# A Conformer's norm issued ahead of the attention, probabilities scaled on GpSimd, evictions issued behind the weight splits

## The chip, the cores and the metric

One core of a Trainium2 chip runs one decoder layer for 256 tokens. The metric is the device time of one execution in microseconds, the median of several runs. TensorE does the matmuls; VectorE, ScalarE and GpSimd do the elementwise work; SP issues most of the loads. Each engine works through its instructions in the order in which the kernel issued them, and waits where one needs the result of another engine.

## What is computed

`x` is 256 x 2048. A layer is an RMS norm, one input projection, two parallel branches, an output projection with a residual, then an RMS norm, a gated MLP with a 3-tap convolution, another residual and a final RMS norm.

```python
proj = rms_norm(x, mix_norm_g) @ w_in
q, kv, gate_logits, conv_in = split(proj)            # 1024, 1536, 48, 2048 columns
attn = nsa_attention(q, kv, sigmoid(gate_logits), ...)
a, gate = split(conv_in)                             # the Conformer's branch
u = causal_depthwise_conv(a * sigmoid(gate), conv_w, conv_b)     # 31 taps, 1024 channels
conv = silu(layer_norm(u, conv_ln_g, conv_ln_b))
x = x + concat(attn, conv) @ w_out
x = x + conv_glu_ffn(rms_norm(x, ffn_norm_g))
return rms_norm(x, final_norm_g)
```

The attention has 16 query heads and three branches for each: over compressed keys, over selected blocks (with 256 tokens there are four blocks, and all are selected) and over a window, which covers everything. Each branch is a softmax with a bias by distance, and a gate.

## The kernel before

**Weights.** They come in 186 chunks of up to 128 x 2048 float32 in the order of their use: 0 to 15 the pairs of gate and value columns of the Conformer (gb and ab of j = 0 to 7), 16 to 19 the keys and values to be compressed, 20 to 23 the keys, 24 and 25 values, 26 to 29 values and gates (narrower, 128 x 1216), 30 to 37 the queries, 38 to 53 the output projection, then the MLP. Chunks 0 and 1 come with x transposed in one packed input, `head`, cut by `CUTS` into pieces. For accuracy each product is made of three matmuls, high x high, high x low and low x high: `w_split` copies a chunk to `wh` in a rounded type on ScalarE (L109) and subtracts for `wl` (L114), in two halves each, on VectorE or, for chunks within `POOLED`, on GpSimd. The last half issues the load of the chunk three further on SP's queue. `w_next` is called at the start of a chunk and queues the pieces of the split of the chunk two further on; `w_pump` issues them.

**Hooks.** A chunk has four hooks between its matmuls (L323). A hook issues one piece of a split, one entry of `steps` and of `conf`, the attention's ticks that `TICKS` names, and then `fill` issues taps of the Conformer's convolution while a clock of planned VectorE time is less than a lead ahead of the planned TensorE time. `mm3`, `mm_rows`, `attn_tick`, `step` and the evictions charge these two clocks. The convolution has 8 x 31 pieces (`side`): one of ScalarE (L358) and 30 taps of VectorE (L363) for each j, between SBUF and one of two halves of PSUM banks.

**Evictions.** After a chunk's matmuls the kernel issues what empties its PSUM bank: `glu_gate` and `glu` for the Conformer, the multiplications for `tok` (L424), the split of the keys (L487 to L494), `v_evac` (L502), `q_evac` (L552 to L557).

**The norm of x.** `xr` is x in rows; `x_rstd` sums squares on ScalarE (L251) and VectorE (L252), GpSimd takes the power -0.5 (L256), `x_diag` and `x_spread` bring it to all partitions (`rB`). It stands behind chunk 0 and 1.

**The attention.** 32 units (8 query pairs, 2 heads, 2 branches) go through a pipeline of ticks: scores (TensorE), minimum with bias (VectorE, L632), exponential (ScalarE, L643), reciprocal times gate (VectorE, L651), scaling (ScalarE, L658) at D_S = 3, transpose (TensorE, L664) into bank 6 and its eviction `es` (ScalarE, L669) at D_T = 4, product with the values (TensorE, L677, L678) at D_T + 1. The compressed branch (`cmp_scores`, `cmp_exp`, `cmp_probs`, `cmp_tr`, which makes `pct`) goes through `steps`.

**The Conformer's norm.** `conf_steps` fills `conf`: sums over channels (VectorE, L713), means by a matmul (L717) and a copy (`ck`, ScalarE, L741), subtraction (L744), squares (L748), sums, variance by a matmul (L724), power on GpSimd (L754), diagonals (L730), spread by a matmul (L733), multiplication. The list starts when no taps are left and `cbst["q"]` says that the first two query chunks are out. `conf2` holds swish and split, issued in the output projection.

## Time and profile before

| | |
|---|---|
| device time, median of 3 runs | 1143.84 us (1143.76 to 1145.13) |
| the profiled execution: device time | 1145.46 us |
| the profiled execution: span from first to last instruction | 1143.3 us |
| mean granted TensorE clock | 0.993 of full speed |

The spans of TensorE's instructions are modelled in part: matmuls overlap, so a stretch can be shown as wholly busy. Times in the rows are microseconds, means of one instruction nanoseconds. PE is TensorE, PEld its weight loads, DVE VectorE, ACT ScalarE, POOL GpSimd.

### The profile page before, as it was taken

What the parts mean: (1) busy time and instruction counts of PE and PEld (TensorE: products, weight loads), DVE (VectorE), ACT (ScalarE), POOL (GpSimd) and SP (SyncE); (2) the same over time, 40 slices, a digit from 0 to 9 for tenths busy, and PEclk for the clock granted to TensorE, in tenths of its full rate; (3) what the DMA queues carried; (4) which work ended last, traced back from release to release, by engine and by line L of the source; (5) the groups of instructions that cost most, each with busy time, mean ns of one, the idle gap of its engine ahead of it and who ended that gap; (6) DMA issues with size and microseconds to landing.
All of it is one profiled execution on the core that took longest, in us unless ns stands there. A gap on an engine that the chain in (4) does not pass through costs nothing.

```text
span 1143.3 us, 16193 instructions
## 1 busy us (share of the span) xinstructions
PE 1116.6 (98%) x6482; PEld 977.6 (86%) x6482; DVE 767.7 (67%) x1250; ACT 598.3 (52%) x898; POOL 128.3 (11%) x80
## 2 busy tenths in 40 slices
PE   8999999899899999999999999999999999999997
PEld 8999999888778888888888888888888888888886
DVE  6688659676454667777777777777778755456554
ACT  6544255788864555544555554455555444444443
POOL 1988654000000000000000000000000000000000
PEclk9999999999999999999999999999999999999999
DMA  9585416222265465555555555555555555555541
GB/s 374 193 299 201 165 45 247 93 75 74 74 237 205 148 234 195 197 184 185 186 190 197 197 187 184 185 189 193 197 194 184 184 184 184 187 183 187 186 177 74
DMA packets 32279, 207.44 MB, mean 181 GB/s; under 512 B 3867, under 2 KB 6187, under 8 KB 8012
## 3 DMA queue, kind: packets, MB, share of 16 engines
q1 hardware_dynamic: 28592, 199.64, 48.9%
q10 hardware_dynamic: 3612, 6.76, 1.6%
q8 instruction: 51, 0.84, 0.3%
q14 instruction: 24, 0.20, 0.1%
HBM read 204.27 MB, written 2.12 MB: 181 GB/s over the span
## 4 chain that ended last, share of the span: by engine, by line
PE 87%; ACT 5%; DVE 4%; DMA 2%; issue 1%; POOL 1%; DVEq 0%; POOLq 0%; ACTq 0%
PE bank L957 28%; PE bank L959 14%; PE bank L145 9%; PE bank L144 9%; PE bank L146 9%; PE bank L139 4%; PE bank L137 4%; PE bank L138 4%; DMA xr<-in_x 2%; ACT wh L109 1%; PE bank L437 1%; ACT e L643 1%; DVE wl L114 1%; PE bank L677 1%; ACT e L658 1%
## 5 line engine op out<-in xcount | busy, mean ns | idle before, releaser
L109 ACT ACTIVATE wh<-wraw 128x2048 fp32r<-128x2048 f32 (+2 forms) x239 | 355.9, 1505 | 356.5 <-issue 149.6
L114 DVE TENSOR_TENSOR wl<-wraw,wh 128x2048 fp32r<-128x2048 f32 (+1 forms) x185 | 362.6, 1968 | 189.8 <-ACT wh L109 189.7
L957 PE MATMUL bank<-xt,wh 128*128 128x512 f32 x1408 | 488.6, 394 | 0.0
L959 PE MATMUL bank<-xt,wl 128*128 128x256 f32 x1408 | 390.0, 277 | 0.0
L957 PEld LDWEIGHTS bank<-xt,wh 128*128 128x128 f32 x1408 | 264.0, 188 | 61.1
L959 PEld LDWEIGHTS bank<-xt,wl 128*128 128x128 f32 x1408 | 264.4, 188 | 0.0
L137 PE MATMUL bank<-xt,wh 128*128 128x256 f32 x512 | 147.8, 289 | 1.7 <-ACT wh L238 1.7
L139 PE MATMUL bank<-xt,wl 128*128 128x256 f32 x512 | 146.3, 286 | 1.9 <-POOL wl L114 1.6
L138 PE MATMUL bank<-xt,wh 128*128 128x256 f32 x512 | 146.1, 285 | 0.0
L144 PE MATMUL bank<-wh,gh 128*128 128x512 f32 (+1 forms) x360 | 140.8, 391 | 0.0
L145 PE MATMUL bank<-wl,gh 128*128 128x512 f32 (+1 forms) x360 | 140.8, 391 | 0.0
L146 PE MATMUL bank<-wh,gl 128*128 128x512 f32 (+1 forms) x360 | 140.8, 391 | 0.0
L114 POOL TENSOR_TENSOR wl<-wraw,wh 128x1024 fp32r<-128x1024 f32 (+1 forms) x54 | 120.9, 2277 | 36.0 <-ACT wh L109 35.6
L137 PEld LDWEIGHTS bank<-xt,wh 128*128 128x128 f32 x512 | 99.0, 193 | 3.5 <-ACT wh L238 2.1
L139 PEld LDWEIGHTS bank<-xt,wl 128*128 128x128 f32 x512 | 99.0, 193 | 2.5 <-POOL wl L114 1.8
L138 PEld LDWEIGHTS bank<-xt,wh 128*128 128x128 f32 x512 | 99.0, 193 | 0.6
L173 POOL TENSOR_TENSOR rstd<-ms,half 128x1 f32<-128x1 f32 x4 | 2.2, 548 | 857.3 <-DVE ms L166 857.3
L363 DVE SCALAR_TENSOR_TENSOR bank<-us,cw,bank 128x256 f32<-128x256 f32 x232 | 93.7, 482 | 4.7 <-ACT bank L358 4.3
L920 DVE SCALAR_TENSOR_TENSOR yt<-u,vecs,yt 128x255 f32<-128x255 f32 (+1 forms) x176 | 80.9, 481 | 3.1
L144 PEld LDWEIGHTS bank<-wh,gh 128*128 128x128 f32 x360 | 67.8, 188 | 15.8
L145 PEld LDWEIGHTS bank<-wl,gh 128*128 128x128 f32 x360 | 67.8, 188 | 15.8
L146 PEld LDWEIGHTS bank<-wh,gl 128*128 128x128 f32 x360 | 67.8, 188 | 15.8
(185 smaller groups left out, 1047.4 us busy)
## 6 DMA issues: line engine op xcount, KB each, us to landing
wraw<-in_w_u SPq DMA_DIRECT2D x88, 1024.0 KB, 4.8
wraw<-in_w_d SPq DMA_DIRECT2D x44, 1024.0 KB, 4.8
wraw<-in_w_t SPq DMA_DIRECT2D x30, 1024.0 KB, 5.0
wraw<-in_w_o SPq DMA_DIRECT2D x16, 1024.0 KB, 4.9
wraw<-in_w_vg SPq DMA_DIRECT2D x4, 608.0 KB, 3.5
hb<-in_head SPq DMA_DIRECT2D x2, 1024.0 KB, 9.8
xr<-in_x SPq DMA_DIRECT2D x2, 1024.0 KB, 16.0
wb<-rel_scratch ACTq DMA_DIRECT2D x1, 2048.0 KB, 10.7
```

The source lines that it names most:

```text
L109: nc.scalar.activation(h[:, sl], raw[:, sl], AF.Copy)
L114: (nc.gpsimd if pooled else nc.vector).tensor_sub(l[:, sl], raw[:, sl], h[:, sl].bitcast(F32))
L137: nc.tensor.matmul(ps, wh, xh, start=first, stop=False)
L138: nc.tensor.matmul(ps, wh, xl, start=False, stop=False)
L139: nc.tensor.matmul(ps, wl, xh, start=False, stop=last)
L144: nc.tensor.matmul(ps, xh, wh, start=first, stop=False)
L145: nc.tensor.matmul(ps, xh, wl, start=False, stop=False)
L146: nc.tensor.matmul(ps, xl, wh, start=False, stop=last)
L363: nc.vector.scalar_tensor_tensor(y[:, j] if last else acc[0], us[:, j, k:k + T], cw[:, j, k:k + 1], acc[0], op0=OP.mult, op1=OP.add)
L920: nc.vector.scalar_tensor_tensor(ys[i][:, d:], us_[i][:, :T - d], fcw[:, c, k:k + 1], ys[i][:, d:], op0=OP.mult, op1=OP.add)
L957: nc.tensor.matmul(bk[i], wh[:, k, sl], xt[:, kt].rearrange("p a t -> p (a t)"), start=kt == 0, stop=False)
L959: nc.tensor.matmul(bk[i][:, :T], wl[:, k, sl], xt_h[:, kt], start=False, stop=kt == KD - 1)
```

## The change

`late` holds evictions: they are now issued by the next chunk's `w_next`, behind the split that it queues; for chunks that GpSimd splits, `w_next` issues the whole split at once. `POOLED` moves from 3..29 to 5..31. `head` has six pieces, and the three first chunks are loaded ahead of the rows of x; three small loads move from ScalarE's queue, behind the norm of x, to SP's, behind its rows. The norm of x is issued behind chunk 2. The Conformer's list starts when the taps are out and the last `glu` is issued, with more empty entries; its functions stand earlier in the text, and are otherwise the same. The scaling is on GpSimd, D_T is 5. The queries' split (`q_split`) is issued behind the first tick of the next chunk, and a hook runs ticks before steps. The charges of the clocks are raised. No matmul is added or taken away.

```diff
-POOLED = (3, 30)
-CUTS = ((0, 2), (2, 4), (4, 8), (8, 12), (12, 16))
+POOLED = (5, 32)
+CUTS = ((0, 2), (2, 4), (4, 6), (6, 8), (8, 12), (12, 16))
...
+    late = []
...
         while st["split"] <= min(c + ahead, len(chunks) - 1):
             w_pump()
             w_split(cuts)
-        if cuts == 1:
+        if cuts == 1 or POOLED[0] <= st["split"] - 1 < POOLED[1]:
             w_pump()
+        now = late[:]
+        late.clear()
+        for f in now:
+            f()
         return parts.pop(c)
...
-        clock["pe"] += 0.32
+        clock["pe"] += 0.36
...
-        clock["pe"] += 0.64
+        clock["pe"] += 0.7
...
         def load_small():
-            nc.scalar.dma_start(oh, a["onehot"])
-            nc.scalar.dma_start(rbn[:32], a["rel_slots"])
-            nc.scalar.dma_start(cw, a["conv_vecs"])
+            nc.sync.dma_start(oh, a["onehot"])
+            nc.sync.dma_start(rbn[:32], a["rel_slots"])
+            nc.sync.dma_start(cw, a["conv_vecs"])
...
-        w_dma()
+        for _ in range(3):
+            w_dma()
         xr = [ap.tile([P, D], F32, name=f"xr{t}", tag=tg) for t, tg in enumerate(("y", "us"))]
         for t in range(2):
             nc.sync.dma_start(xr[t], x_rows[:, t])
-        w_dma()
-        w_dma()
+        load_small()
...
+        behind = []
+        cbst = {"q": 0, "done": 0, "glu": False}
...
                 if conf:
-                    clock["dve"] += 0.4
+                    clock["dve"] += 0.9
                     conf.pop(0)()
...
         def hook(i, ticks={}):
-            if i < 2:
-                w_pump(1)
-            step()
             if i in ticks:
                 for _ in range(ticks[i]):
                     attn_tick()
-            if i >= 2:
-                w_pump(1)
+            while behind:
+                behind.pop(0)()
+            w_pump(1)
+            step()
             fill(1.0 if i in ticks else 0.8 if cbst["q"] else 2.0)
-            if not side and cbst["q"] and "b" not in cf:
+            if not side and cbst["glu"] and "b" not in cf:
                 conf_steps()
...
+                first = gb, ab
+                continue
+            tile_chunk(gb)
+            if j == 1:
                 x_rstd()
...
-                load_small()
-                first = gb, ab
-                continue
-            tile_chunk(gb)
-            if j == 1:
-                steps[:0] = [x_diag, lambda: None, x_spread]
                 tile_chunk(ab)
-                glu(0, first[1], glu_gate(first[0]))
-                glu(1, ab, glu_gate(gb))
+                steps[:0] = [x_diag, x_spread, lambda: glu(0, first[1], glu_gate(first[0])),
+                             lambda gb=gb, ab=ab: glu(1, ab, glu_gate(gb))]
             else:
-                sg = glu_gate(gb)
+                sg = []
+                late.append(lambda gb=gb, sg=sg: sg.append(glu_gate(gb)))
                 tile_chunk(ab)
-                glu(j, ab, sg)
+                late.append(lambda j=j, ab=ab, sg=sg: glu(j, ab, sg[0]))
+        late.append(lambda: cbst.update(glu=True))
...
+        def conf_steps():
+            cf["b"] = bank[6][:, 384:]
+            conf.extend((
+                lambda: None, lambda: conf_sum("y", y, 0, P), lambda: conf_sum("y", y, P, T), lambda: None,
+                lambda: None, lambda: conf_mean(0), lambda: conf_mean(1),
+                lambda: (conf_apply(OP.subtract, 0), conf_sq(0)), lambda: conf_apply(OP.subtract, 4),
+                lambda: (conf_sum("s0", cf["s"]), conf_sq(4)), lambda: None, lambda: conf_sum("s1", cf["s"]),
+                lambda: None, lambda: None, conf_var, conf_rstd, lambda: None, lambda: None,
+                lambda: conf_spread(0), lambda: conf_spread(1), lambda: conf_apply(OP.mult, 0),
+                lambda: conf_apply(OP.mult, 4)))
...
-        for n in range(4):
-            tile_chunk(bank[n][:, :T])
+        def k_evac(n):
             br, q = divmod(n, 2)
             k32 = bank[n][:, :T]
             nc.vector.tensor_mul(k32, k32, rB)
...
                 nc.scalar.activation(k_h[h, r, q, br], k32[h], AF.Copy)
                 nc.vector.tensor_sub(k_l[h, r, q, br], k32[h], k_h[h, r, q, br].bitcast(F32))
+            for r in range(2):
+                h, o = slice(64 * r, 64 * r + 64), slice(64 - 64 * r, 128 - 64 * r)
                 nc.scalar.activation(k_h[o, r, q, br], k32[h], AF.Copy)
                 nc.scalar.activation(k_l[o, r, q, br], k_l[h, r, q, br].bitcast(F32), AF.Copy)
+
+        for n in range(4):
+            tile_chunk(bank[n][:, :T])
+            late.append(lambda n=n: k_evac(n))
...
-        for t in range(2):
-            v_evac(t, 0, vb[t][:, :256])
+        late.extend(lambda t=t, src=vb[t][:, :256]: v_evac(t, 0, src) for t in range(2))
...
-                    clock["pe"] += 0.35
+                    clock["pe"] += 0.42
...
+        late.append(vg_evac)
...
+        def q_split(i):
             for r in range(2):
                 h, o = slice(64 * r, 64 * r + 64), slice(64 - 64 * r, 128 - 64 * r)
                 nc.scalar.activation(qs[h, i % 4, r], q32[i][h], AF.Copy)
                 nc.vector.tensor_sub(qs[o, i % 4, r], q32[i][h], qs[h, i % 4, r].bitcast(F32))
+            split_q.add(i)
...
         def st_scale(n):
             i, r, br = units[n]
             e, lsum = US[n]
             for t, (lo, hi, _) in enumerate(HALVES):
-                nc.scalar.activation(e[:, lo:hi], e[:, lo:hi], AF.Copy, scale=lsum[:, br, t:t + 1])
+                nc.gpsimd.tensor_scalar_mul(e[:, lo:hi], e[:, lo:hi], lsum[:, br, t:t + 1])
...
-        D_S, D_T = 3, 4
+        D_S, D_T = 3, 5
...
             clock["pe"] += 1.4
-            clock["dve"] += 0.85
+            clock["dve"] += 1.1
...
+        def q_out(i):
+            q_evac(i, bank[i % 2])
+            behind.append(lambda: q_split(i))
+            if i % 2:
+                cbst["q"] = i // 2 + 1
+                cmp_branch(i // 2)
+
         for i in range(8):
             if i == 2:
                 fill(1e9)
             tile_chunk(bank[i % 2][:, :T], TICKS[min(i, 2)])
-            q_evac(i, bank[i % 2])
-            if i % 2:
-                cbst["q"] = i // 2 + 1
-                cmp_branch(i // 2)
+            late.append(lambda i=i: q_out(i))
```

## Rows read from the trace of the kernel before

**Rows 1.** The page: busy time of the engines over the span, and its group of the first matmul of a gate chunk (busy us, mean ns of one, then idle time before).

```profile
PE 1116.6 (98%) x6482; PEld 977.6 (86%) x6482; DVE 767.7 (67%) x1250; ACT 598.3 (52%) x898; POOL 128.3 (11%) x80
...
L137 PE MATMUL bank<-xt,wh 128*128 128x256 f32 x512 | 147.8, 289 | 1.7 <-ACT wh L238 1.7
```

**Rows 2.** Busy time by stage: the stretch, its length, then busy us and instructions of each engine, TensorE's granted clock, the DMA engines' share and GB/s.

```profile
0.00:30.00 30.00, 25.39 (x172) 24.35 (x173) 17.92 (x41) 20.39 (x38) 5.41 (x12) 0.94 0.88 358
30.00:130.00 100.00, 100.00 (x830) 99.22 (x830) 81.23 (x205) 43.02 (x53) 87.95 (x40) 1.00 0.64 226
142.00:175.00 33.00, 30.70 (x257) 30.18 (x256) 20.35 (x55) 19.08 (x38) 16.52 (x10) 0.95 0.17 58
175.00:199.00 24.00, 24.00 (x186) 24.00 (x186) 23.22 (x49) 12.57 (x24) 10.30 (x9) 1.00 0.71 252
199.00:305.00 106.00, 95.57 (x663) 87.58 (x662) 71.27 (x240) 88.81 (x261) 1.41 (x5) 0.98 0.22 79
```

**Rows 3.** The same view of the three stretches with a granted clock under 1.

```profile
10.00:20.00 10.00, 9.00 (x60) 8.79 (x61) 9.86 (x18) 10.00 (x20) 0.00 (x0) 0.83 1.01 426
160.00:180.00 20.00, 18.00 (x134) 17.80 (x134) 16.70 (x44) 11.04 (x22) 14.03 (x9) 0.91 0.29 95
220.00:230.00 10.00, 9.51 (x61) 9.17 (x61) 4.52 (x16) 6.45 (x21) 0.00 (x0) 0.83 0.00 0
```

**Rows 4.** What TensorE waited for from 0 to 400 us: who waited for whom, us in total, times, the longest.

```profile
PE bank L677 <- ACT es L669: 3.4, 5, 1.4
PE bank L664 <- ACT ck L741: 3.2, 2, 1.9
PE bank L517 <- POOL wl L114: 2.0, 1, 2.0
PE bank L137 <- ACT wh L238: 1.7, 2, 1.3
PE bank L139 <- POOL wl L114: 1.6, 1, 1.6
PE bank L681 <- ACT pct L598: 1.2, 1, 1.2
...
PE bank L724 <- ACT es L669: 0.9, 1, 0.9
PE bank L717 <- ACT es L669: 0.9, 1, 0.9
```

**Rows 5.** ScalarE from 199 to 305 us, by form: count, then busy us and mean ns of one, then idle time before.

```profile
L658 ACT ACTIVATE e<-e,lsum 128x256 f32<-128x256 f32 x29 | 14.4, 497 | 0.0
L669 ACT ACTIVATE es<-bank 128x384 f32<-128x384 f32 x28 | 13.5, 482 | 8.1 <-PE bank L664 8.1
...
L658 ACT ACTIVATE e<-e,lsum 128x128 f32<-128x128 f32 x29 | 11.4, 394 | 2.5 <-DVE lsum L652 2.3
L556 ACT ACTIVATE qs<-q 64x256 fp32r<-64x256 f32 x14 | 5.8, 412 | 1.1 <-DVE q L552 0.9
...
L748 ACT ACTIVATE s<-y 128x1024 f32<-128x1024 f32 x2 | 2.1, 1058 | 1.6 <-DVE y L744 1.3 <-DVE lsum L651 0.3
```

**Rows 6.** VectorE from 199 to 305 us, the same view.

```profile
L114 DVE TENSOR_TENSOR wl<-wraw,wh 128x1024 fp32r<-128x1024 f32 x16 | 19.5, 1221 | 0.7 <-ACT wh L109 0.7
...
L557 DVE TENSOR_TENSOR qs<-q,qs 64x256 fp32r<-64x256 f32 x14 | 5.9, 420 | 5.2 <-ACT qs L556 5.1
...
L744 DVE TENSOR_TENSOR y<-y,ck 128x1024 f32<-128x1024 f32 x4 | 4.9, 1221 | 0.2 <-ACT ck L741 0.2
L713 DVE TENSOR_REDUCE s<-s 128x256 f32<-128x1024 f32 x2 | 4.1, 2033 | 0.0
L713 DVE TENSOR_REDUCE y<-y 128x128 f32<-128x1024 f32 x2 | 4.0, 2002 | 0.0
```

**Rows 7.** GpSimd over the whole span, by form.

```profile
L114 POOL TENSOR_TENSOR wl<-wraw,wh 128x1024 fp32r<-128x1024 f32 x46 | 109.2, 2410 | 34.6 <-ACT wh L109 34.3
L114 POOL TENSOR_TENSOR wl<-wraw,wh 128x608 fp32r<-128x608 f32 x8 | 11.7, 1508 | 1.3 <-ACT wh L109 1.3
...
L754 POOL TENSOR_TENSOR rv<-rv,half 128x1 f32<-128x1 f32 x2 | 1.1, 560 | 34.6 <-DVE rv L752 34.6
...
L431 POOL MEMSET vc<- 128x512 f32 x1 | 0.5, 529 | 0.0
```

**Rows 8.** In order of time, from the key chunks on: one row of ScalarE, one of VectorE (42 taps in a run, behind the last key eviction), one of GpSimd. Start, length, what, and in brackets the idle time before it and what ended it.

```profile
143.49 0.38 ACT L491 ACTIVATE k_h<-bank 64x256 fp32r<-64x256 f32 x1 [12.96 <-DVE bank L487]
...
171.74 16.55 DVE L363 SCALAR_TENSOR_TENSOR bank<-us,cw,bank 128x256 f32<-128x256 f32 x42
...
166.90 4.68 POOL L114 TENSOR_TENSOR wl<-wraw,wh 128x1024 fp32r<-128x1024 f32 x2 [4.66 <-ACT wh L109]
```

**Rows 9.** The same view around the norm of x: one row of VectorE, one of GpSimd.

```profile
22.44 1.23 DVE L252 CUSTOM_DVE_ANT_0 sqd<-xr 128x1024 bf16<-128x1024 f32 x1 [2.54 <-DMA xr<-in_x]
...
26.82 18.89 POOL L114 TENSOR_TENSOR wl<-wraw,wh 128x1024 fp32r<-128x1024 f32 x8
```

**Rows 10.** The first matmul of each group of three in the value-and-gate chunks: count, duration (least, median, most), first and last start.

```profile
L531 PE MATMUL bank<-wh,xt x32: 297/302/309, 176.5 to 189.5; 128*128 128x304 f32 x32
```

**Rows 11.** In order of time around 55 us: VectorE's multiplication of the small table of biases, and GpSimd's splits beside it.

```profile
55.32 2.19 DVE L283 TENSOR_SCALAR rbn<-rbn 32x16 f32<-32x16 f32 x1
...
50.34 9.51 POOL L114 TENSOR_TENSOR wl<-wraw,wh 128x1024 fp32r<-128x1024 f32 x4
```

More of the change, by code (lines that the diff above doesn't have):

```diff
@@ new lines, in conf_mean, with conf_var, conf_diag @@
+        def conf_mean(t):
+            nc.tensor.matmul(cf["b"], inv_c, cf["y"][:, t * P:(t + 1) * P], start=True, stop=True)
+            conf_keep(t)
+        def conf_var():
+            for t in range(2):
+                for i, name in enumerate(("s0", "s1")):
+                    nc.tensor.matmul(cf["b"][:, t:t + 1], cf[name][:, t * P:(t + 1) * P], inv_c[:, :1],
+                                     start=i == 0, stop=i == 1)
+        def conf_diag(cols):
+            cf["d"] = wk.tile([P, 2, P], F32, name="dg", bufs=1)
+            for t in range(2):
+                nc.vector.tensor_scalar_mul(cf["d"][:, t], ident, cols[:, t:t + 1])
@@ new lines, in conf_spread, with conf_keep, conf_apply @@
+        def conf_spread(t):
+            nc.tensor.matmul(cf["b"], ones, cf["d"][:, t], start=True, stop=True)
+            conf_keep(t)
+            if t:
+                cf["done"] = True
+        def conf_keep(t):
+            if t == 0:
+                cf["k"] = wk.tile([P, T], F32, name="ck", tag="sg")
+            nc.scalar.activation(cf["k"][:, t * P:(t + 1) * P], cf["b"], AF.Copy)
+        def conf_apply(op, j0):
+            nc.vector.tensor_tensor(y[:, j0:j0 + 4], y[:, j0:j0 + 4], cf["k"][:, None].to_broadcast([P, 4, T]), op=op)
@@ new lines, in conf_sq, with conf_rstd, conf_swish @@
+        def conf_sq(j0):
+            cf["s"] = ap.tile([P, 4, T], F32, name="s2", tag="tok")
+            nc.scalar.activation(cf["s"], y[:, j0:j0 + 4], AF.Square)
+        def conf_rstd():
+            rv = wk.tile([P, 2], F32, name="rv", bufs=1)
+            nc.vector.tensor_scalar(rv, cf["b"][:, :2], EPS, None, op0=OP.add)
+            for t in range(2):
+                nc.gpsimd.tensor_tensor(rv[:, t:t + 1], rv[:, t:t + 1], half, op=OP.pow)
+            conf_diag(rv)
+        def conf_swish(j0):
+            for j in range(j0, j0 + 4):
+                nc.scalar.activation(y[:, j], y[:, j], AF.Silu, scale=cw[:, j, TAPS + 1:TAPS + 2],
+                                     bias=cw[:, j, TAPS + 2:TAPS + 3])
@@ L639, in st_exp @@
             if n % 2 == 0:
-                US["l"] = wk.tile([P, 2, 2], F32, name="lsum", bufs=3)
+                US["l"] = wk.tile([P, 2, 2], F32, name="lsum", bufs=4)
             lsum = US["l"]
@@ L702, in attn_tick @@
                 if 0 <= n - d < NU:
[L703 removed]
+                    assert f is not st_scores or n // 4 in split_q
                     f(n - d)
[L707 to L714 removed]
@@ L716, in conf_mean @@
-        def conf_mean(t):
-            nc.tensor.matmul(cf["b"], inv_c, cf["y"][:, t * P:(t + 1) * P], start=True, stop=True)
-            conf_keep(t)
-        def conf_var():
-            for t in range(2):
-                for i, name in enumerate(("s0", "s1")):
-                    nc.tensor.matmul(cf["b"][:, t:t + 1], cf[name][:, t * P:(t + 1) * P], inv_c[:, :1],
-                                     start=i == 0, stop=i == 1)
-        def conf_diag(cols):
-            cf["d"] = wk.tile([P, 2, P], F32, name="dg", bufs=1)
-            for t in range(2):
-                nc.vector.tensor_scalar_mul(cf["d"][:, t], ident, cols[:, t:t + 1])
@@ L732, in conf_spread @@
-        def conf_spread(t):
-            nc.tensor.matmul(cf["b"], ones, cf["d"][:, t], start=True, stop=True)
-            conf_keep(t)
-            if t:
-                cf["done"] = True
-        def conf_keep(t):
-            if t == 0:
-                cf["k"] = wk.tile([P, T], F32, name="ck", tag="sg")
-            nc.scalar.activation(cf["k"][:, t * P:(t + 1) * P], cf["b"], AF.Copy)
-        def conf_apply(op, j0):
-            nc.vector.tensor_tensor(y[:, j0:j0 + 4], y[:, j0:j0 + 4], cf["k"][:, None].to_broadcast([P, 4, T]), op=op)
```

78 lines of the change are left out of this document (27 added, 51 removed).

## The prediction

> **What bounds the kernel now.** I read first the page's busy shares, then the busy time by stage, then the waits of TensorE, then the forms of ScalarE, VectorE and GpSimd in the stages where TensorE waits. TensorE is busy 98% of the span [rows 1]; all matmuls stay, so the change can only give back what TensorE loses. By stage [rows 2] it is idle 4.6 us of the first 30 (about 1 of it before its first instruction), nothing in the gate chunks (30:130), 2.3 in 142:175 (key chunks, value chunks), nothing in 175:199 and 10.4 in the attention (199:305); what is left of its 26.7 idle lies mostly at the end, which no edit touches. Two corrections. A matmul of the gate chunks starts every 0.12 us (830 in 100 us [rows 2]) but is shown 0.29 long [rows 1], so each pause hides some 0.17. And the granted clock is 0.83 in 10:20, 0.91 in 160:180 and 0.83 in 220:230 [rows 3]: at levels of 2.4 and 1.2 GHz each is 3.4 us at the lower, of which half, 1.7 us, is lost. Each comes in or just after a stretch with TensorE idle. All that can be won is then about 4.6 - 1 + 2.3 + 10.4 = 16.3, some 2.5 hidden in about 15 pauses, and 5.1 of clock: 24 us, 2.1%.
>
> In the attention it is ScalarE that sets the pace: 88.8 us busy of 106, against 71.3 of VectorE and 1.4 of GpSimd [rows 2]. The waits of TensorE there end on ScalarE: 3.4 us for `es`, 3.2 for the Conformer's `ck`, 0.9 and 0.9 at its matmuls L717 and L724, 1.2 for `pct` [rows 4].
>
> **The change part by part.**
>
> *Scaling on GpSimd.* ScalarE loses 29 x 0.497 + 29 x 0.394 = 25.8 us in 199:305 [rows 5]. GpSimd's price for 256 and 128 elements has no row. Above: the line through its two-input splits (1024 at 2.410, 608 at 1.508: 2.17 ns an element and 0.19) gives 0.74 + 0.47 = 1.21 us a unit. Below: its memset reads nothing and takes 0.529 for 512, so 0.26 + 0.13 = 0.39 [rows 7]. A scaling reads one tensor, so I take the middle, 0.8. The 28 evictions `es` in 106 us [rows 5] make a tick 3.8 us now; even 1.21 fits three times, and with D_T at 5 the transpose comes two ticks after the scale.
>
> *Conformer's norm out of the attention.* ScalarE loses another 2.1 (squares) [rows 5], VectorE 4.9 + 4.1 + 4.0 = 13.0 [rows 6]. ScalarE then needs 88.8 - 25.8 - 2.1 = 61, VectorE 58, GpSimd 11 to 35, and TensorE 106 - 10.4 - 10 pauses x 0.17 - 1.7 of clock = 92 (the pauses for `es`, `ck`, `pct` and at L717 and L724 [rows 4]): TensorE becomes the bound with a third of the time free on each of the others. What stays: the turn from the first to the second output chunk, where the last compressed branch is issued just ahead of its transposes (`pct`, 1.2), more so now that the hook runs ticks before steps; and jitter. Of 10.4 + 1.7 + 1.7 = 13.8 I leave 2.8: **-11.0**. Bounds: -13.8 if nothing stays, -3 by the third rival.
>
> *Evictions behind splits* (`late`), L517's wait. ScalarE stood 13.0 us before L491, waiting for the key eviction of VectorE that waits for TensorE; the splits behind it were late, GpSimd started the value chunk's at 166.90 [rows 8], and TensorE waited 2.0 us for it [rows 4]. With the splits ahead this goes: 2.3 idle, 0.3 hidden, 1.7 of clock, of which 0.3 stays: **-4.0** (bounds 0 to -4.3). What is late next is the key eviction: VectorE now waits 2.0 us (two halves of 1.05) behind the splits at the first key chunk, and its taps queue behind that.
>
> *The norm of x moved behind the second gate column, chunk 3 split on VectorE.* VectorE stood before `sqd` until the rows of x had landed, at 22.44; GpSimd's rstd came after, and its split of chunk 3 at 26.82 [rows 9], for which TensorE waited 1.6 [rows 4]. Now chunks 3 and 4 are split by VectorE before it waits. The rows of x land behind two more chunks, 2 MB at 426 GB/s (the first of [rows 3], last column), so near 27.5; VectorE's sums and rstd end near 32, and TensorE reaches the spread near 33.5. The three small loads go behind them on SP's queue, before the next chunk's load, and are needed later still. **-1.8** (bounds: 0, if x lands 3 us later than that).
>
> *Six head pieces.* TensorE waited 1.7 in two pauses for ScalarE's part of a piece [rows 4]; smaller third pieces come earlier, but ScalarE's conversions set the end, and the pause partly moves behind the fourth piece. With what the clock may keep: **-1.5** (bounds 0 to -3).
>
> *What the moved norm costs where it lands.* In the gate, key and value chunks the planner's own charges fix where it is issued. There are 248 pieces of taps at 0.4; a chunk now gives 16 x 0.36 = 5.76. From the third hook of chunk 4 to chunk 23, less 7.2 for the gates, 4.0 and 3.9 for evictions and 0.15 a step, that pays for about 227; chunk 24 for 11, chunk 25 for the last 10. (The same sum with the old charges leaves 42 pieces after the last key eviction, and the trace has one run of 42 [rows 8].) So `conf` begins at the last hook of the second value chunk and takes one entry a hook through the four value-and-gate chunks. These are short: 32 groups of three matmuls from 176.5 to 189.5 [rows 10], so 0.42 a group, two groups or 0.84 us a hook, 3.35 a chunk, where a tick of the attention was 3.8. Call the start of the first of them V, and TensorE's arrival without stalls: first mean at V+3.3, variance at V+10.8, first spread at V+15.5 (second hook of the first query chunk).
>
> VectorE from the second key chunk to V: 52 taps at 16.55/42 = 0.394 [rows 8] are 20.5, four key evictions some 7, the wait behind the splits 2.0, the compressed branch 2.4: 32 against 29.3 of TensorE, so it is 2.5 late at V. Then two sums of 2.0 [rows 6] end at V+6.5: the mean stalls 3.2. Two means, copy, two subtractions of 1.22, square 1.06, sum 2.03, square, sum [rows 5, 6] end at V+15.7, where TensorE arrives at 14.0: 1.7. The rstd stands in GpSimd's queue behind the splits of chunks 30 and 31, which POOLED's new upper limit 32 has just put there: 4 x 2.4 = 9.6 us [rows 7] from about V+11.5 to 21.1, two powers of 0.56, two diagonals: V+23.0, where TensorE arrives at 20.4: 2.6. **+7.5**, and one stretch of lower clock, as after the three stalls of before: **+1.7**. Bounds 0 (if VectorE comes early) and +16 (each VectorE operation with two inputs delayed by one GpSimd split of 2.4, and two more stretches).
>
> *Queries split behind the tick, D_T 5, charges.* They move instructions within a hook; the work that hides them is the tick's TensorE work, and without that cover two copies of 0.41 [rows 5] a query pair would show, under 1 us a chunk. One more tick drains in the third output chunk, ahead of the fourth, which first reads its result. 0 (+2 at most).
>
> Sum: -11.0 - 4.0 - 1.8 - 1.5 + 7.5 + 1.7 = **-9.1**. The profiled execution took 1145.46 (span 1143.3, 2.2 around it), 1.6 above the median of 1143.84; against the median, **1135**.
>
> **A shared port.** At 55.32 VectorE took 2.19 us to multiply a tile of 32x16 by -1, while GpSimd ran splits without a gap from 50.34 to 59.85 [rows 11]; its taps (one SBUF tensor, one PSUM) kept 0.394 beside splits [rows 8]. The Trainium skill, "GPSIMD Engine Reference", section 1, says that GpSimd shares VectorE's SBUF interface and collides with operations in a two-port mode or with two SBUF inputs; by that, the weight splits (16 x 1.22), the query splits (14 x 0.42) [rows 6] and the compressed branch would each wait for a scaling, and the trace agrees as far as that one row goes. The same page, section 4.1, would leave elementwise work on VectorE. By these the sum keeps little of its first term, which is the third rival.
>
> **The rivals.**
> 1. The forecast: the attention is freed, the moved norm stalls TensorE in the short chunks. 1135. Chance 0.45.
> 2. The moved norm is covered: VectorE is early at V and GpSimd's queue shorter. Then +9.2 falls away: 1126. For it: no TensorE wait at all in 175:199 now. Against: three serial steps through VectorE, GpSimd and ScalarE in 12 us. 0.24.
> 3. The port: some 45 VectorE operations with two SBUF inputs wait for scalings, 0.3 us on average, up to 0.74, and the scalings for splits of 1.22; the minima come late and the ticks keep their idle. VectorE's 58 + 14 of 92 says it need not; but that is a mean. 3 of the 11 won: 1143. 0.19.
> 4. Slower: GpSimd sets the tick. Without the attention's gain the other terms make +1.9. A tick is 3.79 now; past 3.7 us a unit the kernel is slower, at 4.0 by 28 x 0.21 + 1.9 = 7.8: 1152. That is three times the upper bound from its splits, but a scalar from a pointer on GpSimd has no row. 0.08.
> The remaining 0.04 is for neither.
>
> **How the numbers follow.** A difference of 0.2%, 2.3 us, is what a measurement of this kernel can tell. Faster: 0.45 + 0.24 + nearly half of the third: 0.78. Same: the other part of it, 0.10. Slower: 0.12. The range goes from 1124 to 1144: all of the first case, most of the second, two thirds of the third: 0.8. The first case's own range, from its bounds, is 1130 to 1140.
>
> **What would show it.** L658 on GpSimd, between 0.4 and 1.2 us a unit, and ScalarE under 70% busy in the attention; no TensorE wait for `wl` at chunk 3 or at L517; TensorE waiting at L717's, L724's and L733's successors in the value-and-gate chunks and the first query chunk, the last behind GpSimd's power. It is wrong if the waits of the attention remain (then 3), or if GpSimd's scalings stand in the chain (then 4).

## The result, and the profile after

The changed kernel takes 1135.08 us (1134.13 to 1137.22), where the kernel before took 1144.19 beside it: a ratio of 0.992, 95% interval 0.9905 to 0.9939. The forecast was 1135. Its profiled execution has a span of 1133.4 us against 1143.3.

From the page, busy time over the span, as in [rows 1]:

```profile
PE 1111.6 (98%) x6482; PEld 975.4 (86%) x6482; DVE 768.2 (68%) x1252; ACT 579.3 (51%) x836; POOL 187.0 (17%) x144
```

The number of matmuls is the same. TensorE's busy time fell by 5.0 us, which is time at the lower clock and what pauses hide, and its idle time by the other 4.9. Busy time by stage, as in [rows 2, 3]; the last three lines are single stretches of 10 us:

```profile
0.00:30.00 30.00, 26.84 (x198) 25.93 (x199) 21.55 (x42) 20.78 (x40) 0.69 (x6) 1.00 0.93 378
30.00:130.00 100.00, 100.00 (x826) 98.97 (x825) 89.85 (x233) 44.30 (x53) 86.34 (x42) 1.00 0.64 229
142.00:175.00 33.00, 30.94 (x267) 30.38 (x265) 27.42 (x71) 18.99 (x40) 22.89 (x16) 1.00 0.28 92
175.00:199.00 24.00, 19.26 (x127) 18.98 (x128) 14.24 (x16) 11.30 (x21) 13.52 (x10) 0.86 0.54 194
199.00:305.00 106.00, 102.64 (x732) 95.34 (x731) 66.22 (x244) 74.29 (x209) 59.07 (x68) 1.00 0.28 93
10.00:20.00 10.00, 8.93 (x72) 8.52 (x71) 9.61 (x20) 9.12 (x19) 0.00 (x0) 1.00 1.00 419
170.00:180.00 10.00, 6.02 (x38) 5.77 (x38) 9.53 (x16) 3.74 (x7) 7.87 (x6) 0.83 0.67 230
180.00:190.00 10.00, 9.10 (x57) 9.02 (x55) 6.45 (x4) 6.30 (x7) 4.26 (x2) 0.83 0.21 87
```

The attention (199:305) now idles 3.4 us of TensorE in place of 10.4, with ScalarE at 74 us in place of 89 and GpSimd at 59 in place of 1. The three stretches under full clock of [rows 3] are gone; in their place 175:199, which had no idle at all, idles 4.7 us and runs at 0.86. Where the clock falls differs between runs of the same code: e2, e10 and e11 (below) keep the head of before and have 1.00 in 10:20. What TensorE waited for from 0 to 400 us, as in [rows 4]:

```profile
PE bank L430 <- DVE y L426: 4.0, 1, 4.0
PE bank L685 <- DVE pcb L680: 2.2, 1, 2.2
PE bank L142 <- ACT wh L243: 1.9, 2, 1.0
PE bank L766 <- ACT es L758: 1.1, 2, 0.6
...
PE bank L544 <- DVE hd L533: 1.1, 1, 1.1
...
PE bank L437 <- DVE s L426: 0.9, 1, 0.9
PE bank L446 <- DVE dg L443: 0.8, 1, 0.8
```

Of the waits in [rows 4], those for `ck`, for GpSimd's `wl` (L517 and L139) and for `pct` are gone, and 3.4 us for `es` became 1.1. New are the three of the moved norm: the mean (L430), the variance (L437) and the spread (L446); the transpose of the last compressed branch at the turn to the second output chunk (L685); and the compressed keys (L544).

To have the loss whole, with the clock and what pauses hide, I took for every matmul the time to the next one's start, less the median spacing of that pair's form, and summed the excess by stage (worked out from the starts in both traces):

| stage | before, us | after, us | change | forecast |
|---|---|---|---|---|
| head, 0:20 | 4.7 | 3.5 | -1.2 | -1.5 |
| norm of x, 20:30 | 1.9 | 0 | -1.9 | -1.8 |
| keys and values, 140:170 | 4.7 (to 180) | 1.8 | -2.9 | -4.0 |
| moved norm, 170:200 | 0 | 8.8 | +8.8 | +7.5 and +1.7 |
| attention, 200:310 | 15.5 | 3.1 | -12.4 | -11.0 |
| rest | 0.8 | 0.5 | -0.3 | 0 |
| all | 27.5 | 17.6 | -9.9 | -9.1 |

The sum closes on the change of the span, 9.9 us. The stages depend on how the forms are told apart: with other groupings of the same starts the attention comes out between -9 and -12 and the moved norm between +7 and +9, so that a stage is known to some 2 us.

GpSimd by form, the price that had no row:

```profile
L747 POOL TENSOR_SCALAR e<-e,lsum 128x256 f32<-128x256 f32 x32 | 40.6, 1267 | 0.0
L747 POOL TENSOR_SCALAR e<-e,lsum 128x128 f32<-128x128 f32 x32 | 19.3, 604 | 48.3 <-DVE lsum L741 47.2 <-ACT ec L672 1.1
```

A unit costs 0.604 + 1.267 = 1.87 us, more than the 1.21 that the prediction called its upper bound. GpSimd still stood 47 us waiting for VectorE's reciprocals, so it had time to spare on average. The tick it has to fit is the mean distance of the 32 evictions `es`: 3.34 us before (209.8 to 313.4) and 2.88 after (215.8 to 305.0), not 3.79.

### The profile page after: what moved, and what is told of

Read it like the earlier page. It is cut to its first block, busy times and chain, and to the rows that moved or that the text cites. A ratio compares the mean times of both kernels' runs of the same rounds, so it can differ in the third digit from the quotient of the medians.

```text
span 1133.4 us, 16238 instructions
## 1 busy us (share of the span) xinstructions
PE 1111.6 (98%) x6482; PEld 975.4 (86%) x6482; DVE 768.2 (68%) x1252; ACT 579.3 (51%) x836; POOL 187.0 (17%) x144
## 4 chain that ended last, share of the span: by engine, by line
PE 91%; DVE 4%; ACT 2%; POOL 1%; issue 1%; DMA 1%; SPq 0%; DVEq 0%; POOLq 0%; ACTq 0%
PE bank L976 29%; PE bank L978 14%; PE bank L151 10%; PE bank L149 10%; PE bank L150 10%; PE bank L142 5%; PE bank L144 5%; PE bank L143 4%; DVE bank L368 2%; PE bank L766 1%; PE bank L753 1%; DMA hb<-in_head 1%; PE bank L517 1%; POOL wl L115 1%; PE bank L767 1%
```

## The experiments

Each is timed against the kernel before on the same chip; the ratio is to that. "After" is 1135.1 us, ratio 0.992.

### Which half of the first term is it: the scaling or the norm?

**e1_scale_act**, the scaling back on ScalarE:

```diff
-                nc.gpsimd.tensor_scalar_mul(e[:, lo:hi], e[:, lo:hi], lsum[:, br, t:t + 1])
+                nc.scalar.activation(e[:, lo:hi], e[:, lo:hi], AF.Copy, scale=lsum[:, br, t:t + 1])
```

> The changed kernel with the scaling back on ScalarE; nothing else differs. Theory A (ScalarE set the attention's pace): its 32 x 0.89 = 28 us of scalings come back on top of some 60 in the 92 us from 204 to 296, so it is over 90% busy again, TensorE waits for es as before, and the kernel is 5 to 9 us slower than the changed one: 1140 to 1144, ratio 0.997 to 1.000. Rival B (taking the Conformer's norm and the late evictions out of the attention was enough): within 2 us of the changed kernel, 1135 to 1137.

Measured 1139.87 us, 0.9959 (0.9944 to 0.9974): 4.8 over after (4.2 by the ratios), just under the range of theory A. But the wait that A names did not come back: TensorE waits 0.6 us for `es`, where after has 1.1. What it waits for is the compressed branch:

```profile
PE bank L770 <- ACT pct L687: 2.7, 3, 0.9
PE bank L685 <- DVE pcb L680: 2.7, 1, 2.7
```

With the scalings in its queue ScalarE reaches the copy `pct` late, three times; after has no such wait, and 2.2 us on L685.

**e2_before_pool**, the scaling alone, on the kernel before (with the two buffer counts that a D_T of 5 asks for):

```diff
-                nc.scalar.activation(e[:, lo:hi], e[:, lo:hi], AF.Copy, scale=lsum[:, br, t:t + 1])
+                nc.gpsimd.tensor_scalar_mul(e[:, lo:hi], e[:, lo:hi], lsum[:, br, t:t + 1])
...
-        D_S, D_T = 3, 4
+        D_S, D_T = 3, 5
```

> The kernel before with the scaling alone on GpSimd and D_T at 5. Theory A: the waits for es and one of the lower clock in the attention go, the waits at the Conformer's means, variance and ck (5.0 us of TensorE before) shrink but stay; 6 us faster than before, 1136 to 1140. Rival B: under 2 us faster, 1142 to 1144.

Measured 1148.13 us, 1.0028 (1.0013 to 1.0042): slower than before, against both theories. The size is uncertain: 3.2 us by the ratio, 4.4 by the medians, with eight runs between 1145.49 and 1149.45.

**e3_conf_q**, after with the Conformer's norm started where it was before, beside the ticks:

```diff
-            if not side and cbst["glu"] and "b" not in cf:
+            if not side and cbst["q"] and "b" not in cf:
```

> The changed kernel with the Conformer's list started as before, behind the first two query chunks, so that it runs beside the ticks. Theory A (in the value-and-gate chunks the list costs TensorE 4.0 + 0.9 + 0.8 us of shown waits and 3.4 of lower clock, in all some 9): those go, and beside the ticks, with ScalarE a third free and 3 us a hook, it costs 1 to 4: 5 to 8 us faster than the changed kernel, 1127 to 1130. Rival C (beside the ticks the list costs what it costs in the short chunks): 1134 to 1137.

Measured 1139.66 us, 0.9953 (0.9938 to 0.9968): 4.6 over after (3.5 by the ratios), against both.

The attention of the three, 199:305, in the order e1, e2, e3 (busy us of TensorE, weight loads, VectorE, ScalarE, GpSimd, then the clock):

```profile
199.00:305.00 106.00, 99.97 (x699) 92.37 (x698) 62.53 (x241) 91.27 (x268) 0.38 (x3) 0.98 0.26 90
```

```profile
199.00:305.00 106.00, 92.67 (x634) 85.56 (x632) 68.76 (x228) 68.47 (x192) 49.28 (x60) 0.95 0.22 78
```

```profile
199.00:305.00 106.00, 93.45 (x635) 84.18 (x635) 69.50 (x237) 68.65 (x199) 58.24 (x68) 0.98 0.20 72
```

TensorE idles 6.0, 13.3 and 12.6 us, against 10.4 before [rows 2] and 3.4 after. In e2 and e3 ScalarE lost 20 us of its 89 and the ticks became worse: so relieving ScalarE was not enough. The two largest waits of TensorE in e2's attention:

```profile
PE bank L664 <- POOL e L658: 3.9, 2, 2.8
PE bank L677 <- ACT es L669: 3.2, 4, 1.8
```

The first looks like a price of GpSimd and is not one. The longer of its two, in order of time, GpSimd, then ScalarE, then TensorE:

```profile
254.58 1.51 POOL L658 TENSOR_SCALAR e<-e,lsum 128x128 f32<-128x128 f32 x2
259.50 4.02 POOL L658 TENSOR_SCALAR e<-e,lsum 128x128 f32<-128x128 f32 x4 [3.41 <-DVE lsum L652]
...
261.37 0.85 ACT L556 ACTIVATE qs<-q 64x256 fp32r<-64x256 f32 x2 [0.77 <-DVE q L552]
262.24 1.06 ACT L109 ACTIVATE wh<-wraw 128x1024 fp32r<-128x1024 f32 x1
263.21 0.26 ACT L741 ACTIVATE ck<-bank 128x128 f32<-128x128 f32 x1
...
263.61 0.87 PE L664 MATMUL bank<-ident,e 128*128 128x128 f32 x3 [2.82 <-POOL e L658]
```

Counted in order, the transposes at 263.61 are those of the 14th unit. Its two scalings are the first row here and had ended at 256.09; the four from 259.50 on belong to the 15th and 16th, and the profile names them because the last of them ends just before TensorE starts. The transposes write into bank 6, which held the norm's spread until ScalarE's copy `ck` ended at 263.47. The other of the two waits, at 219.75, lies in the same way behind a `ck` that ends at 219.60, while its unit's scaling had ended at 215.34. So these are the waits for `ck` of [rows 4], 3.2 us there and 3.9 here, and those for `es` are 3.2 for 3.4: with 20 us less to do, ScalarE still comes to both copies late, here because `ck` stands in its queue behind the queries' split, which waits for VectorE, and a weight conversion. Besides, smaller waits grew (1.8 us for 0.9 at L717), and the granted clock is 0.95 in this stretch for 0.98.

In e3 no wait of TensorE names GpSimd. The norm's matmuls (L430, L437, L446) wait 2.8 us for `es` to leave bank 6, the products 3.8 for `es`.

What is shown, then: on the kernel before, the scaling on GpSimd costs about 3 us (e2); on the kernel after, it saves 4 to 5 (e1); and on the kernel after, the norm's place saves some 4 (e3), though it costs 8.8 in the chunks where it now lies. That it is the norm's place which turns the sign of the scaling's price is likely and not shown: before and after also differ in the order within a hook, the queries' split and the late evictions, and after with the norm beside the ticks and the scaling on ScalarE was not run.

### The moved norm's stalls

**e4_conf_gaps**, after with more empty entries between the steps of the norm, so that each matmul comes later behind the VectorE work that it needs:

```diff
-                lambda: None, lambda: conf_sum("y", y, 0, P), lambda: conf_sum("y", y, P, T), lambda: None,
-                lambda: None, lambda: conf_mean(0), ...
+                gap(1) + [lambda: conf_sum("y", y, 0, P), lambda: conf_sum("y", y, P, T)] + gap(6)
+                + [lambda: conf_mean(0), ...] + gap(4) + [conf_var, conf_rstd] + gap(2) + ...
```

> The changed kernel with more empty entries in the Conformer's list: the mean four hooks later (six empty entries behind the sums instead of two), the variance two and the spread six hooks later than now, so that it reaches into the first ticks. Theory A: the mean, variance and spread no longer stall TensorE, the lower clock does not come, and the kernel is 7 to 9 us faster than the changed one: 1126 to 1128. Rival D (what stalls is VectorE and GpSimd being late as such; a later place only moves the stall): 1132 to 1136.

Measured 1132.44 us, 0.989 (0.9873 to 0.9906), in rival D's range. The norm's waits fell from 5.7 us to 1.4, all of it on the mean, and 175:199 ran at full clock. But the first ticks paid: TensorE waited 2.1 us at 208. GpSimd in order of time there, then VectorE:

```profile
203.48 5.78 POOL L748 TENSOR_SCALAR e<-e,lsum 128x128 f32<-128x128 f32 x4 [7.27 <-DVE lsum L742]
209.20 0.12 POOL L664 MEMSET ec<- 128x32 f32 x1
...
209.36 0.28 DVE L671 TENSOR_REDUCE mnc<-ec 128x8 f32<-128x120 f32 x1 [1.11 <-POOL ec L664]
```

A fill of 0.12 us for the compressed scores, which the change left on GpSimd, now stands behind four scalings. VectorE waits for it, and the next reciprocal and the next exponential wait behind VectorE. The stretch that follows, 210:220, is granted 0.83.

**e9_gaps_turn_memset** tests this, with the fill on VectorE and the edit of e5 (below) on top of e4:

```diff
-            nc.gpsimd.memset(e[:, 0, :, NC0:], BIG)
+            nc.vector.memset(e[:, 0, :, NC0:], BIG)
```

> The kernel after with three edits: the empty entries of e4_conf_gaps, the earlier compressed branch of e5_turn, and the fill of the compressed scores (L664) on VectorE in place of GpSimd, where in e4_conf_gaps it stood behind four scalings of 5.8 us and held VectorE 1.1 us, ScalarE 3.65 us and TensorE 2.1 us. Theory A (the three waits are separate, and the one of e4_conf_gaps came from GpSimd's queue): 1128 to 1130.5 us, that is e4_conf_gaps less about 2.2 of the turn and 2 of the first ticks. Rival B (the ticks are late there by VectorE's load, not by GpSimd's queue): the wait of L767 for es stands, and the time is 1130.5 to 1132.5 us.

Measured 1127.06 us, 0.9851 (0.9836 to 0.9866): below the range of A, 8.0 under after and the fastest kernel here. It is 5.4 us under e4; less the 2.6 of e5's own run, that leaves some 2.8 for the fill, if the two add. The trace agrees: the wait for `es` falls from 2.8 to 1.7 us, which is 1.1, and 210:220 is back at full clock, which is 1.7. By stage:

```profile
175.00:199.00 24.00, 22.58 (x175) 22.03 (x175) 20.09 (x25) 15.43 (x28) 15.98 (x10) 1.00 0.68 246
199.00:305.00 106.00, 103.63 (x713) 95.13 (x712) 65.64 (x242) 73.01 (x209) 60.52 (x64) 1.00 0.31 110
```

No stretch of 10 us is under full clock any more (the mean over the span is 0.999).

**e12_pool30**, after with GpSimd splitting two chunks fewer:

```diff
-POOLED = (5, 32)
+POOLED = (5, 30)
```

> The kernel after (1135.1 us) with the same edit alone: GpSimd splits chunks 5 to 29, VectorE 30 and 31. Theory A (in the kernel after the reciprocal root just gets through behind the splits of GpSimd: VectorE waits 5.02 us for it and TensorE 0.8): the wait of L446 (0.8 us) goes, and the time is 1133.5 to 1135 us. Rival B (the four splits on VectorE, 4.9 us, come in ahead of the norm's sums and the first ticks): 1136 us or more.

Measured 1134.12 us, 0.9916 (0.9901 to 0.993). The 1.0 us is under what a measurement can tell; the trace says more. In after, GpSimd splits chunks 30 and 31 from 185.74 on and takes the norm's power only then:

```profile
185.74 9.45 POOL L115 TENSOR_TENSOR wl<-wraw,wh 128x1024 fp32r<-128x1024 f32 x4 [7.87 <-ACT wh L110]
195.14 1.08 POOL L467 TENSOR_TENSOR rv<-rv,half 128x1 f32<-128x1 f32 x2
```

In e12 it runs at 190.54, as soon as VectorE has the variance, and the wait of L446 is gone:

```profile
190.54 1.08 POOL L467 TENSOR_TENSOR rv<-rv,half 128x1 f32<-128x1 f32 x2 [13.25 <-DVE rv L465]
```

### The turn to the second output chunk

**e5_turn**, one empty entry less in the last compressed branch:

```diff
-                        (cmp_scores, cmp_exp, lambda m: None, cmp_probs, cmp_tr))]
+                        (cmp_scores, cmp_exp, cmp_probs, cmp_tr))]
```

> The kernel after, with one empty entry less in the list of the last compressed branch (scores, exponential, probabilities, transpose), so that its transpose is issued half a chunk behind its probabilities and not right behind them at the turn to the second output chunk. In the profile after, that transpose (L685) waited 2.2 us for VectorE's probabilities. Theory A (the wait is the distance between the two issues, nothing else): the wait goes and the time is 1132 to 1133.5 us, 1.5 to 3 under the kernel after (1135.1). Rival B (VectorE is simply late there, by its load at the end of the ticks): the wait stands, in the same place or under another name, and the time is 1134.5 to 1136.

Measured 1132.5 us, 0.9891 (0.9877 to 0.9906): theory A. The wait of L685 (2.2 us) is gone; 0.7 us for `mn` is the next in its place. That is 1.5 of the 2.6 us; 175:199, which the edit does not touch, was at 0.93 here and at 0.86 in after.

### Evictions behind the splits

**e6_k_at_once**, the key evictions issued at once as before:

```diff
-            late.append(lambda n=n: k_evac(n))
+            k_evac(n)
```

> The kernel after, with the four evictions of the keys issued at once, ahead of the splits of the next weight chunk, as before; everything else as after. Theory A (evictions ahead of the splits hold the next chunk's weights up, the prediction's term of -4.0): the wait of L544 for hd (1.1 us) goes, but TensorE waits for split weights at the turns between the key chunks by about 2 us, as in rows 7, perhaps with a stretch at the lower clock: 1136 to 1139 us. Rival B (the place of these evictions is worth nothing, or the order only exchanges one wait for another): 1134 to 1135.5 us.

Measured 1136.54 us, 0.9926 (0.9911 to 0.9941). By the ratio that is no difference from after. Its waits of TensorE show an exchange:

```profile
PE bank L430 <- DVE y L426: 2.2, 2, 1.6
PE bank L540 <- DVE hd L533: 2.2, 1, 2.2
PE bank L544 <- DVE hd L533: 1.7, 1, 1.7
```

In the keys' stage TensorE waits 2.8 us more than in after (3.9 for `hd` in place of 1.1), and 142:175 is granted 0.90; in exchange the mean, L430, waits 1.8 less and the clock stays up in 175:199. No split weight is waited for, so neither theory holds as put. But the mechanism of theory A is there, and ends elsewhere (GpSimd, then VectorE):

```profile
144.47 4.71 POOL L115 TENSOR_TENSOR wl<-wraw,wh 128x1024 fp32r<-128x1024 f32 x2 [13.51 <-ACT wh L110]
149.11 0.47 POOL L532 MEMSET hd<- 64x128 f32 x2
...
149.35 0.27 DVE L533 SCALAR_TENSOR_TENSOR hd<-bank,hb,sgm 64x60 f32<-64x60 f32 x1 [2.19 <-POOL hd L532]
```

With the key eviction ahead of the conversion in ScalarE's queue, GpSimd stands 13.5 us for `wh`, as it did before (13.4). The late splits still come in time; the fill of `hd`, which the kernel issues to GpSimd behind them, does not.

### GpSimd's scaling twice as dear

**e7_scale_twice**:

```diff
-                nc.gpsimd.tensor_scalar_mul(e[:, lo:hi], e[:, lo:hi], lsum[:, br, t:t + 1])
+                for by in (1.0, lsum[:, br, t:t + 1]):
+                    nc.gpsimd.tensor_scalar_mul(e[:, lo:hi], e[:, lo:hi], by)
```

> The kernel after, with each scaling on GpSimd preceded by one by 1.0 of the same block, so that GpSimd's work per unit doubles from about 1.9 us to 3.1 to 3.8. Theory A (the unit has two ticks from its reciprocal to its transpose, and GpSimd has time to spare in the attention): the time stays within 2 us of the kernel after, 1134.5 to 1137. Rival B (GpSimd is already close to setting the tick; the prediction put the point at 3.7 us a unit): TensorE's transposes wait for GpSimd, and the time is 1142 us or more.

Measured 1156.43 us, 1.0103 (1.0086 to 1.012): 21 over after, rival B. A unit took 0.61 + 0.95 + 0.69 + 1.05 = 3.30 us by the mean of its four forms. That is over the tick of after, 2.88; the evictions `es` now lie 3.48 apart (216.6 to 324.3), and in 220:300 GpSimd is busy 72.6 of 80 us. So GpSimd sets the tick, and its time alone makes (3.30 - 2.88) x 31 = 13 of the 21 us, an estimate from these figures. The rest comes by way of its queue. VectorE's waits from 199 to 330 us:

```profile
DVE mnc L670 <- POOL ec L663: 14.4, 4, 4.4
...
DVE e L721 <- POOL e L748: 3.9, 2, 2.7
```

and TensorE's in the same stretch:

```profile
PE bank L767 <- DVE lsum L740: 8.6, 3, 3.0
PE bank L754 <- POOL e L748: 3.6, 5, 1.5
```

The same small fill as in e4 stands behind scalings four times: VectorE waits 14.4 us for it, the reciprocals and then the outputs (L767) are late behind that, and GpSimd itself stands 9.9 us for the reciprocals. Only 3.6 us are transposes that wait for a scaling.

### The early edits

**e8_x_norm_head**, the head in five pieces and the norm of x at its old place, in after:

```diff
-CUTS = ((0, 2), (2, 4), (4, 6), (6, 8), (8, 12), (12, 16))
+CUTS = ((0, 2), (2, 4), (4, 8), (8, 12), (12, 16))
...
                 w_pump()
+                x_rstd()
                 first = gb, ab
...
```

> The kernel after, with two early edits undone: the head is loaded and split in five pieces as before, and the first norm's reciprocal root, its spread and the first two gates are issued where they were before. Everything from the third channel chunk on is as after. Theory A (both terms of the prediction, 1.8 and 1.5 us, are real and nothing later takes them up): TensorE's waits in the first 30 us grow by about 3 us and the time is 1137.5 to 1140 us. Rival B (the later stages absorb it, or only one of them counts): 1135 to 1137.

Measured 1152.63 us, 1.0062 (1.0043 to 1.0081): 17.5 over after, far outside both. VectorE in order of time:

```profile
27.28 1.22 DVE L257 CUSTOM_DVE_ANT_0 sqd<-xr 128x1024 bf16<-128x1024 f32 x1 [7.42 <-DMA xr<-in_x]
```

After loads the rows of x behind three weight chunks, where before had them behind one. At the old place VectorE waits 7.4 us for them, with the splits of chunks 3 and 4, now VectorE's own, queued behind. The first 50 us run at a granted clock of 0.86, and TensorE waits 4.9 us for the Conformer's spread later on, as in e10 below. The undo had left its partner, the order of the loads, in place.

**e10_early_as_before** puts the loads back too (the three small ones also return to ScalarE's queue):

```diff
-        for _ in range(3):
-            w_dma()
+        w_dma()
         xr = ...
-        load_small()
+        w_dma()
+        w_dma()
...
```

> The kernel of e8_x_norm_head with the order of the first transfers as before as well: x's rows ahead of two of the three early weight chunks, and the small tables on ScalarE's queue behind the first pair of chunks. So the head, the first norm and their loads are all as before, and from the third channel chunk on all is as after. Theory A (e8_x_norm_head lost its 17 us to x's rows, which came behind three weight chunks, with VectorE waiting 7.4 us for them; the two terms themselves are 3 us, with some for the clock): 1137.5 to 1141 us. Rival B (the first norm is dear in the new order whatever the loads, because the splits of chunks 3 and 4 are now on VectorE behind it): 1143 us or more. Rival C (the terms are worth nothing): 1135 to 1136.5 us.

Measured 1141.28 us, 0.9978 (0.9968 to 0.9988), just over A's range. But its trace says that A is only part of it: the first 40 us lose 2.0 more than in after, and 4.9 us are a wait of TensorE at 192, for the norm's spread. GpSimd there:

```profile
187.27 9.34 POOL L115 TENSOR_TENSOR wl<-wraw,wh 128x1024 fp32r<-128x1024 f32 x4 [2.54 <-ACT wh L110]
196.55 1.10 POOL L469 TENSOR_TENSOR rv<-rv,half 128x1 f32<-128x1 f32 x2
```

The variance reached VectorE 1.35 us earlier than in after (189.20 against 190.55) and the splits started 1.5 us later, so VectorE had to wait 7.8 us for the power in place of 5.0.

**e11_early_pool30**, the same with `POOLED = (5, 30)`:

> The kernel of e10_early_as_before (1141.3 us) with GpSimd splitting weight chunks 5 to 29 only, so that chunks 30 and 31 are split on VectorE. In e10_early_as_before the variance's reciprocal root on GpSimd stood behind four splits of these chunks (9.34 us), VectorE waited 7.8 us for it, and the spread L448 held TensorE 4.9 us, with a clock of 0.73 in that stretch. Theory A (GpSimd's queue is the cause): the wait of L448 goes or falls under 1 us, and the time is 1134.5 to 1137 us. Rival B (the norm's chain is late there for another reason, or VectorE with four more splits of 1.22 us is late in its place): 1139 us or more.

Measured 1135.68 us, 0.9927 (0.991 to 0.9943): theory A. The wait of the spread is gone, and 5.6 us with it. e11 against e12 is then the price of the early edits, with POOLED at 30 in both: 1135.68 - 1134.12 = 1.6 us. That is under the 2.3 that a measurement can tell, though the four runs of each do not overlap (1134.90 to 1135.80, 1133.75 to 1134.70).

## Why the prediction was right

The time came out to 0.1 us. That closeness is luck: the four runs of after go from 1134.13 to 1137.22, and the errors of the terms have both signs. By the table each stage is within 1.4 us of its terms, with stages known to some 2. The moved norm and the attention bear the sum, and both are of the forecast's kind and size. Several reasons under them failed, and did not show because there was slack.

*Attention, -11.0; measured -12.4.* The size was right and the reason half of it. "It is ScalarE that sets the pace" fails as a matter of load: e2 took 20 us off ScalarE, and the waits for `ck` and `es` stayed. They hang on when ScalarE's queue comes to a copy. In after they are gone because the norm, which shares bank 6 with the transposes, has left (e3 brings most of them back), and the lighter ScalarE pays at `pct` (e1). The two edits had been put in one term; the scaling is worth -4.8 on the kernel after and about +3 on the kernel before. Had only the scaling been changed, the same working would have forecast a gain where there was a loss. What was said to stay, the last compressed branch at the turn, stayed: 2.2 us on L685, which e5 removed.

*GpSimd's price, 0.8 a unit in bounds 0.39 to 1.21; measured 1.87.* The upper bound failed. The scaling reads one tensor, and yet costs 0.60 and 0.92 us when VectorE runs no work with two SBUF inputs beside it (below): 2.48 ns an element and 0.29 fixed, no cheaper than a two-input split (2.17 and 0.19). With the waits beside such work the mean is 1.87. It held nothing up in after, where the transposes of a unit come 0.5 to 5.4 us behind the end of its scalings.

*The tick, 3.8.* It was 28 evictions in 106 us; but in the first 10.8 us of that stretch there is none, and the 32 lie 3.34 apart.

*Rival 3, the port.* Its mechanism is real and it falls on the other side: GpSimd waits, and VectorE's splits in the attention take 1.239 us on average where they took 1.221 [rows 6].

*Rival 4.* Its mechanism is what e7 shows, and its point was too high: at 3.30 us a unit the kernel is 11 us slower than before and 21 slower than after, where the rival had the loss begin at 3.7. The step that failed is the tick that the price was held against, 3.79 from the stalled kernel before, where the kernel after goes at 2.88. And GpSimd works in order, so that what stands behind the scalings (a fill, a power, the next pair) is late before its time is used up, as e4 shows.

*The moved norm, +7.5 and +1.7; measured +8.8.* The place (value-and-gate chunks) and the three waits are as forecast. The mean waited 4.0 for 3.2 forecast, the variance 0.9 for 1.7, the spread 0.8 for 2.6. The clock fell in two stretches of 10 us for the one forecast, 3.4 us for 1.7; e1, e5 and e7, with nearly the same three waits, lost 1.7 in 170:190, so that here the forecast had the usual size. The spread was overrated because both sides come later than forecast, GpSimd's power by 3.5 us (its end at V + 25.7, with V at 170.5) and TensorE by 4.4 (V + 24.8): the waits were in its arrival, the lost clock was not. e10 shows 4.9 us for the same queue with a shift of some 3 us. That the power stands behind POOLED's new chunks is shown by e11 and e12.

*Evictions, -4.0; measured -2.9.* The wait for `wl` at L517 went with its dip of the clock. That dip need not come: e2 has the same 2.0 us of wait and full clock in 142:175. "What is late next is the key eviction" came true: VectorE's part of it now waits 1.8 us behind the splits on ScalarE, for 2.0 forecast, and TensorE 1.1 at L544. e6 shows the mechanism (13.5 us for `wh`) for the four key evictions, and that these are worth little here: what the keys' stage gains by them, the norm's mean and its clock lose. The other late evictions were not tested by themselves.

*Early edits, -3.3; the stages show -3.1, and e11 against e12 1.6.* The half for the six head pieces is not shown. TensorE's wait for `wh` there is 1.2 to 2.2 us in the kernels with six pieces and 1.4 to 1.7 in those with five; the -1.2 of the table goes with the dip of the clock in 10:20, which e2, e10 and e11 do not have with five either. The half for the norm of x is borne out: its wait of 1.6 us went, and e11, with the norm back at its place, waits 0.8 for `wl` and 0.5 for the spread of x there. Some 0.7 of it is given back in the Conformer's norm, whose waits are 4.1 us in e11 and 4.8 in e12.

## What to carry to other kernels

Relieving the busiest engine pays only where its load makes it late: here 20 us less changed little, because the order of its queue set when it came to what others waited for. Hold the price of moved work against the tick of the kernel after, which is shorter than the stalled one before, and look at what stands behind it in the queue of the engine that takes it: small fills and powers, since one of 0.12 us cost some 2.8 us here. Do not trust the name of a wait alone; look up when the unit's own input was done. Two edits put into one term should be priced apart as well, because each alone may have the other sign. An early edit shifts the phase of everything later, so undo it together with its loads and read the price from the trace's stages as well as from the total.

## What the runs showed of the hardware

Two units of after, GpSimd's two scalings of each (count, then shortest, median and longest in ns: the 128 columns and the 256). The first is at 256.9, with no work on VectorE that reads two SBUF tensors; the second at 247.7, with VectorE's row below:

```profile
L747 POOL TENSOR_SCALAR e<-e,lsum x2: 603/763/923, 256.9 to 257.4; 128x128 f32<-128x128 f32 x1, 128x256 f32<-128x256 f32 x1
...
L747 POOL TENSOR_SCALAR e<-e,lsum x2: 608/1238/1867, 247.7 to 248.3; 128x128 f32<-128x128 f32 x1, 128x256 f32<-128x256 f32 x1
...
248.14 1.22 DVE L115 TENSOR_TENSOR wl<-wraw,wh 128x1024 fp32r<-128x1024 f32 x1
```

The scaling of 256 that starts inside VectorE's split takes 1.867 us in place of 0.923, that is about what is left of the split (1.08) on top of its own time; the split takes its usual 1.22. Of the 32 scalings of 256 columns, 13 start inside a split and take 1.65 to 1.98 us; the others take 0.92 or 0.93. Where a scaling of 256 had started 0.12 us before it, the split was the one that lengthened, but only to 1.43:

```profile
224.05 1.43 DVE L115 TENSOR_TENSOR wl<-wraw,wh 128x1024 fp32r<-128x1024 f32 x1
```

The Trainium skill, "SBUF — State Buffer", section "SBUF: two separate sides", says that whichever of the two starts first gets the port pair for its whole instruction and the other blocks. By that, the trace agrees for GpSimd; for VectorE it agrees in direction and not in size, since the split began 0.12 us after a scaling of 0.93 and lost 0.21, and splits that began 0.28 to 0.54 us after a scaling of 128 columns (0.60) kept 1.22 or 1.23. The same skill's "GPSIMD Engine Reference", section 1, names the collision that [rows 11] had shown at VectorE's cost; by these runs GpSimd pays most of it.
